# A two-layer encoder: the first layer's operands from a feature-major copy of x, first loads on two queues, first products k-tile by k-tile

## The chip, the core and the metric

The kernel runs on one core of a Trainium2 chip. The core's engines each take their own instruction stream in order and wait for one another through semaphores: PE (TensorE, the matrix engine, with PEld for its weight loads), DVE (VectorE), ACT (ScalarE), POOL (GpSimd) and SP (SyncE, which here only issues DMAs; ACT issues a few as well). The metric is the device time of one execution in microseconds. Before the change it is 609.68 us, the median of three runs (608.34 to 611.04).

## What is computed

The reference is two layers on 256 tokens of 1024 features, all float32. Layer 0 mixes tokens by differential attention, layer 1 by a sparse attention with an indexer; each is followed by a squared-ReLU MLP of width 4096. Only the start of layer 0 matters here:

```
for i in range(DEPTH):
    h = rms_norm(x, norm_mix[i])
    ...
        mix = diff_attention(h, diff_w_in[j], ...)   # q, k, v = split(h @ w_in); rms_norm and rotary on q, k
    x = x + mix
    x = x + sq_relu_mlp(rms_norm(x, norm_mlp[i]), mlp_w1[i], mlp_w2[i])
```

The kernel applies the row scale of rms_norm after the product with the weights, so the product itself needs only x times the gain of each feature, with features on partitions.

## The kernel before

**Split products.** Every float32 operand is split into a high part `hi` (a copy in the matrix engine's reduced format, on ACT, L146 for weights) and a remainder `lo` (on DVE, L147). `mm3` (L150 to L156) multiplies `hi*hi`, `hi*lo` and `lo*hi` into one accumulator, so each 128 x 128 piece of activations against 512 weight columns costs three matmuls (L151, L153, L155). They are called main matmuls below.

**Weights** come in units of 128 x 2048 numbers (1 MB): `unit` issues the DMA on SP and splits the unit in pieces. Three raw buffers and four split buffers rotate, so a DMA waits until DVE has split the unit that is three ahead. The units are called u0, u1, ... in the order of use.

**The start.** `make_h` transposes x, 128 x 128 at a time, on PE (L228, 16 of them), and ACT (L232) and DVE (L234) write the two halves of h from PSUM, times the feature gain. x arrives in four DMAs between the pieces of u0. Warm-up matmuls on zeros (`warm`, L91) run before and between. ACT's queue carries `pack` (gains, identity matrix, constants) and the positions `posi`.

**The first attention layer.** Four groups a0 to a3 of heads; each is one block of 48 main matmuls on two units (`project`: four k-tiles for the first 128 tokens, the same four for the others, then the second unit), followed by two blocks for v. The work on a group's result (`qk_post` and `diff_probs`) runs as a side job: sums of squares (ACT L366, DVE L367), rsqrt (L173 to L179), rotary (L352 to L355), transposes to qkT (PE L384), scores (PE L400, DVE L411), exponentials (ACT L422), difference of the two softmaxes (DVE L594), transposes to keys (PE L429), products with v (PE L436 to L438) and transposes to the next operand (PE L623, from `on`, ACT L618). The output projection begins with main matmul 289.

**Rotary angles** are a chain of some 40 tiny operations on POOL (`rope_angles`, L263 to L316). `rope_sines` takes their sines on ACT (L326 to L328), loads the table for the exponentials (L330) and so stands before every rsqrt of the layer.

**Row scale.** `row_scale` squares x on ACT (L200) and finishes on DVE.

**Order.** A scheduler sets the order of each engine's stream when the program is built; on the chip every engine takes its stream in order. So a change in the first block also shifts where later transposes stand among the main matmuls.

Of the kernel before, what the change touches and what calls it, by code (L numbers as in the profile page):

```python
# [9 lines left out]
F32 = mybir.dt.float32  # L10
F32R = mybir.dt.float32r
I32 = mybir.dt.int32
AF = mybir.ActivationFunctionType
OP = mybir.AluOpType
AX = mybir.AxisListType

D = 1024
# [8 lines left out]
C_NORM = 0  # L26
# [2 lines left out]
C_CQ = 37  # L29
C_ROPE = 40  # L30
C_INV = 120
C_ID = 128
C_LAM = 256
C_END = 512

INV_FREQ = [1.0, 0.1939227432012558, 0.03760603070259094, 0.007292664609849453,
            0.0014142135623842478, 0.00027424818836152554, 5.3182957344688475e-05, 1.0313385246263351e-05]
# [5 lines left out]


@with_exitstack
def trunk(ctx: ExitStack, tc: tile.TileContext, x_in, pos_in, pack_in, wf, out):
    nc = tc.nc
    E = ctx.enter_context
    const = E(tc.tile_pool(name="const", bufs=1))
# [8 lines left out]
    mm = nc.tensor.matmul  # L58
# [4 lines left out]
    def wk():  # L63
        return psum.tile([128, 512], F32, name="wk", bufs=4)


    x = [const.tile([128, D], F32, name=f"x{t}") for t in range(2)]
    pack = const.tile([128, C_END], F32, name="pack")
    posi = const.tile([128, 2], I32, name="posi")

    def load_x(t, n):
        nc.sync.dma_start(x[t][:, n * 512:(n + 1) * 512], x_in[t * 128:(t + 1) * 128, n * 512:(n + 1) * 512])

    nc.scalar.preload_act_table_set("trig_and_small")
    load_x(0, 0)
    nc.scalar.dma_start(pack[:, :C_LAM], pack_in[:, :C_LAM])
    nc.scalar.dma_start(posi, pos_in)

    ident = pack[:, C_ID:C_ID + 128]
    cmask = const.tile([128, 384], F32, name="cmask")  # L80
    vt = const.tile([128, 2, D], F32, name="vt")
    nc.vector.memset(vt[:, 0, :128], 0.0)
    nc.gpsimd.memset(cmask, 0.0)
    nc.gpsimd.memset(cmask[0:64, 64:128], BIG)
    nc.gpsimd.memset(cmask[0:64, 320:384], BIG)


    def warm(n):
        ps = wk()
        for _ in range(n):  # L90
            mm(ps[:, :128], vt[:, 0, :128], vt[:, 0, :128], start=True, stop=True)  # L91

    warm(7)


    def pause(stage):
# [31 lines left out]
    off = [0]  # L128
    split = []

    def unit(cols=2048, dmas=1, pieces=1, between=None):
        raw = wraw.tile([128, 2048], F32, name="raw")
        hi = wsp.tile([128, 2048], F32R, name="whi")
        lo = wsp.tile([128, 2048], F32R, name="wlo")
        src = bass.AP(tensor=wf.tensor, offset=wf.offset + off[0], ap=[[cols, 128], [1, cols]])
        off[0] += 128 * cols
        step = cols // dmas
        for i in range(dmas):
            c = slice(i * step, (i + 1) * step)
            nc.sync.dma_start(raw[:, c], src[:, c])  # L140
            if between is not None and i == 0:
                between()
        step = cols // pieces
        for i in range(pieces):
            c = slice(i * step, (i + 1) * step)
            split[:] = [nc.scalar.activation(hi[:, c], raw[:, c], AF.Copy).ins]  # L146
            nc.vector.tensor_tensor(lo[:, c], raw[:, c], hi[:, c].bitcast(F32), op=OP.subtract)  # L147
        return hi[:, :cols], lo[:, :cols]

    def mm3(ps, ah, al, wh, wl, first, last):  # L150
        mm(ps, ah, wh, start=first, stop=False)  # L151
        tick()
        mm(ps, ah, wl, start=False, stop=False)  # L153
        tick()
        mm(ps, al, wh, start=False, stop=last)  # L155
        tick()  # L156
# [62 lines left out]
    behind = []  # L219
# [16 lines left out]
    def lhs(h, kt, t):  # L236
        hi, lo = h[kt // 4][:2]
        c = slice(t * 128, t * 128 + 128)
        return hi[:, kt % 4, c], lo[:, kt % 4, c]

    def project(ps, h, parts, n):

        nk = sum(p[2] for p in parts)
        k0 = 0
        for wh, wl, cnt in parts:
            wh = wh.rearrange("p (k n) -> p k n", n=n)
            wl = wl.rearrange("p (k n) -> p k n", n=n)
            for t in range(2):
                for i in range(cnt):
                    k = k0 + i  # L250
                    ah, al = lhs(h, k, t)
                    mm3(ps[t], ah, al, wh[:, i], wl[:, i], k == 0, k == nk - 1)
            k0 += cnt

    def quad(us):
        return [(wh, wl, 4) for wh, wl in us]
# [5 lines left out]
    def rope_angles():  # L262
        ve = nc.gpsimd  # L263
        posf = const.tile([128, 2], F32, name="posf")
        ve.tensor_copy(posf, posi)
        shp = [128, 2, 8]
        ang = const.tile(shp, F32, name="ang")
        for t in range(2):
            ve.tensor_scalar(ang[:, t], pack[:, C_INV:C_INV + 8], posf[:, t:t + 1], None, op0=OP.mult)
        tp = const.tile(shp, F32, name="tp")  # L270
        n = const.tile(shp, F32, name="rn")
        nh = const.tile(shp, F32, name="rnh")

        def take(v, m, c):
            ve.tensor_scalar(tp, m, c, None, op0=OP.mult)  # L275
            ve.tensor_tensor(v, v, tp, op=OP.subtract)  # L276

        def whole(o, v, c):
            ve.tensor_scalar(o, v, c, RND, op0=OP.mult, op1=OP.add)
            ve.tensor_scalar(o, o, RND, None, op0=OP.subtract)  # L280

        two_pi = 2.0 * math.pi

        a2 = const.tile(shp, F32, name="a2")
        whole(a2, ang, 2.0 ** -24)
        take(ang, a2, 2.0 ** 24)

        c1 = math.floor(two_pi * 2 ** 9) / 2 ** 9
        c2 = math.floor((two_pi - c1) * 2 ** 21) / 2 ** 21
        whole(n, ang, 1.0 / two_pi)  # L290
        ve.tensor_scalar(nh, n, 1.0 / 2048, RND, op0=OP.mult, op1=OP.add)
        ve.tensor_scalar(nh, nh, RND, 2048.0, op0=OP.subtract, op1=OP.mult)
        nl = const.tile(shp, F32, name="rnl")
        ve.tensor_tensor(nl, n, nh, op=OP.subtract)
        for c in (c1, c2):
            take(ang, nh, c)
            take(ang, nl, c)
        take(ang, n, two_pi - c1 - c2)

        b1 = math.floor(two_pi * 2 ** 14) / 2 ** 14  # L300

        def wrap(v):
            whole(n, v, 1.0 / two_pi)
            take(v, n, b1)
            take(v, n, two_pi - b1)

        k24 = -0.8939688666801969
        kh = math.floor(k24 * 2 ** 12) / 2 ** 12
        b = const.tile(shp, F32, name="rb")
        ve.tensor_scalar(b, a2, kh, None, op0=OP.mult)  # L310
        wrap(b)
        ve.tensor_tensor(ang, ang, b, op=OP.add)
        take(ang, a2, kh - k24)
        wrap(ang)
        lim = 3.1415925
        ve.tensor_scalar(ang, ang, lim, -lim, op0=OP.min, op1=OP.max)  # L316
        return ang, b
# [212 lines left out]


    h = new_h()
    make_h(h, C_NORM, 0, 0)
    warm(4)
    ua = [unit(dmas=4, pieces=4, between=lambda: load_x(0, 1))]
    make_h(h, C_NORM, 0, 1)
    for n in range(2):
        load_x(1, n)
        make_h(h, C_NORM, 1, n)
    ua.append(unit(dmas=2, pieces=4))  # L540
    nc.sync.dma_start(pack[:, C_LAM:], pack_in[:, C_LAM:])
    srow, s2 = row_scale(1)
    angles = rope_angles()
    s2c = const.tile([128, 2], F32, name="s2c0")
# [85 lines left out]
    ready = []  # L630

    def pair():
        return [unit(pieces=2) for _ in range(2)]

    def take():
        return ready.pop(0) if ready else pair()
# [2 lines left out]
    probs, outs = [], []  # L639
    for j in range(4):  # L640
        ps = [acc() for _ in range(2)]
        project(ps, h, quad(take() if j else ua), 512)
        if j == 0:
            ready.append(pair())
            rope_sines(*angles)
            lam()
        probs.append(spawn(diff_probs(ps, pr[j], f"a{j}")))
# [5 lines left out]
    h = new_h()  # L653
# [3 lines left out]
    h = h1  # L657
# [184 lines left out]
def _tiles(w):  # L842

    k, n = w.shape[0] // 128, w.shape[1]
    return w.reshape(k, 128, n).transpose(1, 0, 2).reshape(-1)
# [48 lines left out]
def _pack(i):  # L894

    p = np.zeros((128, C_END), np.float32)
    for n, name in ((0, "norm_mix"), (1, "norm_mlp")):
        for layer in range(2):
            c = C_NORM + 16 * layer + 8 * n
            p[:, c:c + 8] = i[name][layer].reshape(8, 128).T  # L900
    heads = [i[n][0] for n in ("diff_q_norm", "diff_k_norm", "dsa_q_norm", "dsa_k_norm")]
    for c, g in enumerate(heads):
        for r in (0, 64):
            p[r:r + 16, C_GT + c] = 1.0
            p[r + 16:r + 64, C_GT + c] = g[16:]
        p[:, C_ROPE + 16 * c:C_ROPE + 16 * c + 16] = g[:16]
    p[:, C_ROPE + 64:C_ROPE + 80] = 1.0
    p[:, C_SUB] = i["diff_subln"][0]
    p[:, C_CQ:C_CQ + 2] = i["dsa_cq_norm"][0].reshape(2, 128).T
    p[:, C_INV:C_INV + 8] = np.array(INV_FREQ, np.float32)  # L910
    p[:, C_ID:C_ID + 128] = np.eye(128, dtype=np.float32)
    for n, name in enumerate(("q1", "k1", "q2", "k2")):
        p[:, C_LAM + 64 * n:C_LAM + 64 * n + 64] = i["diff_lam_" + name][0]
    return p
# [21 lines left out]
```

## Time and profile before

| what | value |
|---|---|
| median of three runs | 609.68 us (608.34 to 611.04) |
| the profiled execution | 610.02 us |
| its span, first to last instruction | 607.4 us |
| PE busy | 593.5 us |
| DVE, ACT, POOL busy | 428.1, 368.9, 19.1 us |

2.6 us of the profiled execution lie outside its span. Matmuls are pipelined, so a busy PE may still be slowed by what it waits for between two of them: the starts of successive matmuls tell more than the busy time. In the steady state main matmuls start 0.23 us apart. The chain that ended last follows the work back from the last instruction, at each step to what released it.

### The profile page before, as it was taken

To read this page: it belongs to the slowest core of one execution; us is meant where nothing else is said; L and a number is where in the kernel's file an instruction comes from. 1 tells how busy PE (TensorE), PEld (TensorE's weight loads), DVE (VectorE), ACT (ScalarE), POOL (GpSimd) and SP (SyncE) were. 2 spreads that over 40 slices of the span, in tenths; PEclk is the share of its full clock that TensorE was granted. 3 is DMA by queue.
4 is the path that set the end of the run, shared out by engine and by line. 5 is a ranking of instruction groups with operands and counts; after the bars stand their busy time and mean duration, and the time that the engine had idled before them with its cause. 6 is when DMAs were issued, how large, how long until landed. Compare 5 with 4: busy or idle time off the path is not lost.

```text
span 607.4 us, 8479 instructions
## 1 busy us (share of the span) xinstructions
PE 593.5 (98%) x3072; PEld 488.2 (80%) x3072; DVE 428.1 (70%) x1067; ACT 368.9 (61%) x720; POOL 19.1 (3%) x53
## 2 busy tenths in 40 slices
PE   8989999999999999999999899999999999999997
PEld 6767678888888888888787686778888888888886
DVE  5799986579557557656598999766786565666552
ACT  6789987576445444445397589784854454455430
POOL 5600000000000000000000000000000000000000
PEclk9999999999999999999999899999999999999999
DMA  8753453335645564555453226424465555555301
GB/s 311 261 207 145 143 199 132 146 139 209 208 169 183 203 201 161 193 208 169 162 208 140 71 69 209 139 69 140 139 240 185 199 208 177 179 199 206 141 1 70
DMA packets 16025, 102.29 MB, mean 168 GB/s; under 512 B 1904, under 2 KB 2416, under 8 KB 4336
## 3 DMA queue, kind: packets, MB, share of 16 engines
q1 hardware_dynamic: 15696, 101.62, 47.4%
q8 instruction: 24, 0.39, 0.3%
q10 hardware_dynamic: 288, 0.13, 0.1%
q14 instruction: 17, 0.14, 0.1%
HBM read 100.70 MB, written 1.05 MB: 168 GB/s over the span
## 4 chain that ended last, share of the span: by engine, by line
PE 81%; DVE 10%; ACT 3%; POOL 3%; issue 3%; DVEq 0%; POOLq 0%; ACTq 0%
PE wk L479 18%; PE acc L153 15%; PE acc L155 15%; PE acc L151 15%; PE wk L480 9%; DVE wlo L147 4%; DVE s L411 2%; PE wk L429 2%; PE acc L479 1%; PE wk L400 1%; PE wk L228 1%; POOL ang L276 1%; PE wk L384 1%; POOL tp L275 1%; ACT whi L146 1%
## 5 line engine op out<-in xcount | busy, mean ns | idle before, releaser
L147 DVE TENSOR_TENSOR wlo<-raw,whi 128x1024 fp32r<-128x1024 f32 (+2 forms) x210 | 230.0, 1116 | 115.7 <-ACT whi L146 115.5
L146 ACT ACTIVATE whi<-raw 128x1024 fp32r<-128x1024 f32 (+2 forms) x210 | 197.9, 975 | 96.2 <-issue 46.1
L153 PE MATMUL acc<-wlo,act 128*128 128x512 f32 (+1 forms) x504 | 198.8, 394 | 0.6 <-DVE wlo L147 0.6
L151 PE MATMUL acc<-whi,act 128*128 128x512 f32 (+1 forms) x504 | 199.1, 395 | 0.1
L155 PE MATMUL acc<-whi,act 128*128 128x512 f32 (+1 forms) x504 | 198.5, 394 | 0.0
L479 PE MATMUL wk<-act,whi 128*128 128x512 f32 x480 | 169.8, 398 | 0.0
L480 PE MATMUL wk<-act,wlo 128*128 128x256 f32 x480 | 134.7, 281 | 0.0
L155 PEld LDWEIGHTS acc<-whi,act 128*128 128x128 f32 x504 | 95.3, 189 | 19.9 <-issue 1.7
L153 PEld LDWEIGHTS acc<-wlo,act 128*128 128x128 f32 x504 | 95.4, 189 | 19.7 <-DVE wlo L147 1.3
L151 PEld LDWEIGHTS acc<-whi,act 128*128 128x128 f32 x504 | 95.2, 189 | 19.5 <-issue 1.0
L479 PEld LDWEIGHTS wk<-act,whi 128*128 128x128 f32 x480 | 90.1, 188 | 22.0
L480 PEld LDWEIGHTS wk<-act,wlo 128*128 128x128 f32 x480 | 90.7, 189 | 0.5
L488 ACT ACTIVATE act<-on 128x256 fp32r<-128x256 f32 x64 | 26.3, 417 | 57.5 <-DVE on L487 57.5
L422 ACT ACTIVATE s<-s,nb,rs_r 128x128 f32<-128x128 f32 x64 | 34.2, 537 | 6.0 <-DVE nb L420 5.9
L489 DVE TENSOR_TENSOR act<-on,act 128x256 fp32r<-128x256 f32 x64 | 26.8, 424 | 14.5 <-ACT act L488 12.7
L485 ACT ACTIVATE sq<-wk 128x256 f32<-128x256 f32 x60 | 22.4, 375 | 17.6 <-PE wk L480 17.6
L487 DVE SCALAR_TENSOR_TENSOR on<-sq 128x256 f32<-128x256 f32 x64 | 26.6, 421 | 0.9
L486 DVE TENSOR_TENSOR sq<-wk,sq 128x256 f32<-128x256 f32 x60 | 24.9, 418 | 0.0
L232 ACT ACTIVATE act<-wk,pack 128x128 fp32r<-128x128 f32 x64 | 18.5, 377 | 8.1 <-PE wk L228 8.0
L234 DVE SCALAR_TENSOR_TENSOR act<-wk,pack,act 128x128 fp32r<-128x128 f32 x64 | 17.7, 344 | 3.6 <-ACT act L232 3.6
L429 PE MATMUL wk<-pack,s 128*128 128x128 f32 x72 | 15.7, 290 | 2.5 <-DVE s L594 1.7
L527 DVE SCALAR_TENSOR_TENSOR x<-acc,rows,x 128x256 f32<-128x256 f32 x16 | 7.0, 479 | 15.0 <-PE acc L155 15.0
(176 smaller groups left out, 435.6 us busy)
## 6 DMA issues: line engine op xcount, KB each, us to landing
raw<-in_w SPq DMA_DIRECT2D x91, 1024.0 KB, 4.8
x<-in_x SPq DMA_DIRECT2D x4, 256.0 KB, 4.5
raw<-in_w SPq DMA_DIRECT2D x4, 256.0 KB, 5.2
raw<-in_w SPq DMA_DIRECT2D x2, 512.0 KB, 5.8
raw<-in_w SPq DMA_DIRECT2D x1, 984.0 KB, 4.6
raw<-in_w SPq DMA_DIRECT2D x1, 840.0 KB, 4.8
out_dram<-x SPq DMA_DIRECT2D x3, 256.0 KB, 2.0
out_dram<-x SPq DMA_DIRECT2D x2, 128.0 KB, 1.7
```

The lines of the kernel that those rows point to most:

```text
L146: split[:] = [nc.scalar.activation(hi[:, c], raw[:, c], AF.Copy).ins]
L147: nc.vector.tensor_tensor(lo[:, c], raw[:, c], hi[:, c].bitcast(F32), op=OP.subtract)
L151: mm(ps, ah, wh, start=first, stop=False)
L153: mm(ps, ah, wl, start=False, stop=False)
L155: mm(ps, al, wh, start=False, stop=last)
L422: nc.scalar.activation(p[:, TS[t]], s[:, TS[t]], AF.Exp, bias=nb[:, t:t + 1], scale=nsc[:, t:t + 1], accum_out=z[t])
L429: nc.tensor.transpose(pt[:, i * 128:(i + 1) * 128], p[:, i * 128:(i + 1) * 128], ident)
L479: mm(ps.rearrange("p (a b) -> p a b", b=256), wh[:, k, c], both[:, :, k % 4], start=k == 0, stop=False)
L480: mm(ps[:, 256:], wl[:, k, c], hi[:, k % 4], start=False, stop=k == 7)
L487: nc.vector.scalar_tensor_tensor(q, r, 0.0, r, op0=OP.max, op1=OP.mult)
L488: nc.scalar.activation(uh[:, m], q, AF.Copy)
L489: nc.vector.tensor_tensor(ul[:, m], q, uh[:, m].bitcast(F32), op=OP.subtract)
```

## The change

The host lays out a second copy of x by features (`in_xt`, k-tile after k-tile, 256 tokens each) and puts the positions into `pack`, whose part that is needed first shrinks to 130 columns (the identity follows later). `first_h` makes both halves of a k-tile of h straight from that copy in SBUF, one ACT and one DVE instruction for all 256 tokens (128 x 256), with no transposes; the copy lies in the buffer of `vt`, which is free until the v blocks. A quarter of u0 is loaded on ACT's queue, and the rest of u0, u1 and the copy alternate on SP's. The ACT split of each weight quarter is tied behind the activation of the same k-tile (`each`). `project` takes the first block k-tile by k-tile, both token halves of each. u2 (`ahead`) is requested before x itself, which now comes in two loads of 512 KB and is needed for its squares and for the residual only; then follow the rest of `pack` and u3.

```diff
-    nc.scalar.dma_start(pack[:, :C_LAM], pack_in[:, :C_LAM])
-    nc.scalar.dma_start(posi, pos_in)
+    xt = vt.rearrange("p a b -> p (a b)")
+    def load_xt(k0, k1):
+        nc.sync.dma_start(xt[:, k0 * 256:k1 * 256], xt_in[:, k0 * 256:k1 * 256])
+    load_xt(0, 2)
+    nc.scalar.dma_start(pack[:, :C_ID], pack_in[:, :C_ID])
...
-    warm(7)
+    for _ in range(8):
+        mm(ps[:, :128], zero, zero, start=True, stop=True)
...
+            with tc.issue_after(each(i)) if each is not None else ExitStack():
+                split[:] = [nc.scalar.activation(hi[:, c], raw[:, c], AF.Copy).ins]
...
+            for t, i in ([(t, i) for i in range(cnt) for t in range(2)] if by_k else
+                         [(t, i) for t in range(2) for i in range(cnt)]):
...
-    make_h(h, C_NORM, 0, 0)
-    warm(4)
-    ua = [unit(dmas=4, pieces=4, between=lambda: load_x(0, 1))]
-    make_h(h, C_NORM, 0, 1)
-    for n in range(2):
-        load_x(1, n)
-        make_h(h, C_NORM, 1, n)
-    ua.append(unit(dmas=2, pieces=4))
-    nc.sync.dma_start(pack[:, C_LAM:], pack_in[:, C_LAM:])
+    def first_h(k):
+        hi, lo, _ = h[k // 4]
+        v, g = xt[:, k * 256:(k + 1) * 256], pack[:, C_NORM + k:C_NORM + k + 1]
+        with tc.issue_after(split[0]) if split else ExitStack():
+            behind[:] = [nc.scalar.activation(hi[:, k % 4], v, AF.Copy, scale=g).ins]
+        nc.vector.scalar_tensor_tensor(lo[:, k % 4], v, g, hi[:, k % 4].bitcast(F32), op0=OP.mult, op1=OP.subtract)
+        return behind[0]
+    ua = [unit(dmas=((nc.scalar, 0, 1, None), (nc.sync, 1, 2, lambda: load_xt(2, 4)),
+                     (nc.sync, 2, 4, lambda: load_xt(4, 8))), pieces=4, each=first_h)]
+    ua.append(unit(dmas=((nc.sync, 0, 1, None), (nc.sync, 1, 2, None)), pieces=4, each=lambda i: first_h(4 + i)))
+    ahead = unit(pieces=2)
+    for t in range(2):
+        nc.sync.dma_start(x[t], x_in[t * 128:(t + 1) * 128, :])
+    nc.sync.dma_start(pack[:, C_ID:], pack_in[:, C_ID:])
...
-        project(ps, h, quad(take() if j else ua), 512)
+        project(ps, h, quad(take() if j else ua), 512, by_k=j == 0)
         if j == 0:
-            ready.append(pair())
+            ready.append([ahead, unit(pieces=2)])
```

Three places show how the streams move; the rows name line, operation, result and inputs, and lines after the change are three or eleven higher. First PE, from the warm-up into the first block. Before:

```order
L91 MATMUL wk<-vt 128x128 x7
L228 MATMUL wk<-pack,x_79 128x128 x4
L91 MATMUL wk<-vt 128x128 x4
L228 MATMUL wk<-pack,x_79 128x128 x4
L151 MATMUL acc<-whi,act 128x512
L153 MATMUL acc<-wlo,act 128x512
L155 MATMUL acc<-whi,act 128x512
```

PE at the same place, after:

```order
L93 MATMUL wk<-zero 128x128 x8
L154 MATMUL acc<-whi,act 128x512 x2
L156 MATMUL acc<-wlo,act 128x512
L158 MATMUL acc<-whi,act 128x512
```

The transposes are gone, here and between the next main matmuls, and the first two products serve both token halves from one weight piece.

Second ACT, from the end of x's squares (L200, after: L203) over the sines (L326, L329) to the first rsqrt of a0 (`rs_y`). Before:

```order
L200 ACTIVATE qn,rowss<-x_80 128x1024
L364 ACTIVATE qn<-acc 128x512
L146 ACTIVATE whi<-raw 128x1024 x2
L366 ACTIVATE sq<-qn 128x512
L364 ACTIVATE qn<-acc 128x512
L146 ACTIVATE whi<-raw 128x1024 x2
L326 ACTIVATE sn<-ang 128x2x8
L327 ACTIVATE rb<-ang 128x16
L366 ACTIVATE sq<-qn 128x512
L328 ACTIVATE cs<-rb,hp 128x2x8
L330 ACT_TABLE_LOAD
```

ACT at the same place, after:

```order
L149 ACTIVATE whi<-raw 128x1024 x2
L203 ACTIVATE qn,rowss<-x_79 128x1024
L203 ACTIVATE qn,rowss<-x_80 128x1024
L367 ACTIVATE qn<-acc 128x512 x2
L369 ACTIVATE sq<-qn 128x512 x2
L149 ACTIVATE whi<-raw 128x1024 x2
L329 ACTIVATE sn<-ang 128x2x8
L330 ACTIVATE rb<-ang 128x16
L331 ACTIVATE cs<-rb,hp 128x2x8
L333 ACT_TABLE_LOAD
```

Both token halves' copies and sums of squares now stand ahead of u3's split and of the sines; u2's split has moved ahead of x's squares.

Third PE at the end of the attention stage, around the transposes of `on` (L623, after: L634). Before:

```order
L623 MATMUL wk<-pack,on 128x128
L155 MATMUL acc<-whi,act 128x512
L623 MATMUL wk<-pack,on 128x128 x2
L151 MATMUL acc<-whi,act 128x512
L623 MATMUL wk<-pack,on 128x128 x2
L153 MATMUL acc<-wlo,act 128x512
L623 MATMUL wk<-pack,on 128x128
```

PE at the same place, after:

```order
L158 MATMUL acc<-whi,act 128x512
L634 MATMUL wk<-pack,on 128x128 x5
L439 MATMUL wk<-vt,aT 128x128
L634 MATMUL wk<-pack,on 128x128
L440 MATMUL wk<-vt,aT 128x128
L634 MATMUL wk<-pack,on 128x128 x2
```

They stood among the last eight main matmuls of the second v block, and stand behind all of them now. Main matmuls counted up to each helper: the first transposes of a0 move from 106 to 110, its scores from 117 to 122; scores and first keys of a3 from 243 and 262 to 254 and 268, its second keys from 265 to 276. Beyond the attention stage the streams are the same.

## Rows read from the trace of the kernel before

**Rows 1.** The page: the span, and the shares of the chain that ended last.

```profile
span 607.4 us, 8479 instructions
...
PE 81%; DVE 10%; ACT 3%; POOL 3%; issue 3%; DVEq 0%; POOLq 0%; ACTq 0%
```

**Rows 2.** Busy time by engine in stretches from the span's start (PE, PEld, DVE, ACT, POOL, with the number of instructions; then the granted clock, DMA share and GB/s).

```profile
30.00:50.00 20.00, 17.43 (x90) 13.43 (x90) 20.00 (x64) 17.83 (x37) 0.00 (x0) 1.00 0.60 220
...
130.00:140.00 10.00, 10.00 (x60) 8.81 (x60) 7.65 (x16) 7.79 (x16) 0.00 (x0) 1.00 0.60 210
```

**Rows 3.** What PE waited for between 7 and 100 us (us in total, times, longest).

```profile
PE wk L384 <- DVE qn L355: 2.2, 1, 2.2
PE wk L429 <- DVE s L594: 1.7, 4, 0.5
```

**Rows 4.** The timeline of PE (start, duration, instruction). Main matmuls 0, 14, 48, 49 and 105 by their place in the stream, then the first transposes of a0 and, behind main matmul 109, the next six.

```profile
7.10 0.48 PE L151 MATMUL acc<-whi,act 128*128 128x512 f32 x1
...
12.33 0.40 PE L155 MATMUL acc<-whi,act 128*128 128x512 f32 x1
...
20.15 0.39 PE L151 MATMUL acc<-whi,act 128*128 128x512 f32 x1
20.84 0.50 PE L153 MATMUL acc<-wlo,act 128*128 128x512 f32 x1 [0.30 <-DVE wlo L147]
...
33.68 0.39 PE L151 MATMUL acc<-whi,act 128*128 128x512 f32 x1
36.23 0.44 PE L384 MATMUL wk<-pack,qn 128*128 128x128 f32 x2 [2.16 <-DVE qn L355]
...
37.44 0.82 PE L384 MATMUL wk<-pack,qn 128*128 128x128 f32 x6
```

**Rows 5.** The chain that ended last, between 0 and 37 us (start, duration, what).

```profile
1.43 4.63 issue
...
10.79 0.22 POOL rnh L291
...
13.38 1.49 POOL ang L276
...
25.31 0.21 POOL ang L316
25.55 0.22 ACT sn L326
...
29.66 1.23 DVE wlo L147
```

**Rows 6.** The timeline of ACT: a square of x, the first half's sum of squares of a0, the split of u3, the sines.

```profile
13.63 1.07 ACT L200 ACTIVATE qn<-x 128x1024 f32<-128x1024 f32 x1
...
20.05 0.62 ACT L366 ACTIVATE sq<-qn 128x512 f32<-128x512 f32 x1
...
21.05 2.00 ACT L146 ACTIVATE whi<-raw 128x1024 fp32r<-128x1024 f32 x2
25.55 0.22 ACT L326 ACTIVATE sn<-ang 128x16 f32<-128x16 f32 x1 [2.50 <-POOL ang L316]
```

**Rows 7.** DMA issues (result, queue, number, KB each, us from issue to landing): the two on ACT's queue, issued at 0.75 and 1.18 us; the first quarter of u0, issued at 1.17 us; u2, issued at 7.66 us. Then what moved from 4 to 4.5 us and from 7 to 8 us.

```profile
pack<-in_pack ACTq DMA_DIRECT2D x1, 128.0 KB, 3.2
posi<-in_pos ACTq DMA_DIRECT2D x1, 1.0 KB, 4.9
...
raw<-in_w SPq DMA_DIRECT2D x1, 256.0 KB, 4.7
...
raw<-in_w SPq DMA_DIRECT2D x1, 1024.0 KB, 8.1
...
DMA packets 57, 0.06 MB, mean 123 GB/s; under 512 B 27, under 2 KB 27, under 8 KB 57
...
DMA packets 225, 0.40 MB, mean 404 GB/s; under 512 B 28, under 2 KB 28, under 8 KB 225
```

**Rows 8.** Groups of instructions in the first 20 us, shapes kept apart (number, then busy us and mean ns of one), with the 1024-column split from 7 to 35 us.

```profile
L146 ACT ACTIVATE whi<-raw 128x512 fp32r<-128x512 f32 x8 | 4.9, 641 | 3.9 <-DMA raw<-in_w 3.9
L147 DVE TENSOR_TENSOR wlo<-raw,whi 128x512 fp32r<-128x512 f32 x8 | 5.4, 692 | 3.1 <-ACT whi L146 3.0
L232 ACT ACTIVATE act<-wk,pack 128x128 fp32r<-128x128 f32 x16 | 5.0, 372 | 0.2
...
L147 DVE TENSOR_TENSOR wlo<-raw,whi 128x1024 fp32r<-128x1024 f32 x8 | 9.6, 1220 | 1.2 <-ACT whi L146 1.2
```

**Rows 9.** The timeline of PE at the end of the attention stage: scores of a3, its last key transposes, the first transposes of `on`, the last product with v.

```profile
80.77 1.58 PE L400 MATMUL wk<-qkT 64*128 64x128 f32 x16
...
88.89 0.44 PE L429 MATMUL wk<-pack,s 128*128 128x128 f32 x2
...
95.50 0.33 PE L623 MATMUL wk<-pack,on 128*128 128x128 f32 x1
...
100.81 0.39 PE L438 MATMUL wk<-vt,aT 128*128 128x128 f32 x2
```

**Rows 10.** The timeline of ACT there: the eight scalings that make `on`.

```profile
95.08 2.18 ACT L618 ACTIVATE on<-wk,rs_r 128x128 f32<-128x128 f32 x8
```

**Rows 11.** Busy time and granted clock (third number from the end) around the idle stretch of PE in the second layer, columns as in rows 2.

```profile
343.30:345.20 1.90, 0.00 (x0) 0.01 (x1) 1.90 (x11) 0.00 (x0) 0.00 (x0) 1.00 0.18 73
345.20:348.70 3.50, 3.47 (x10) 2.82 (x11) 3.50 (x14) 1.96 (x4) 0.00 (x0) 0.51 0.02 5
```

More of the change, by code (lines that the diff above doesn't have):

```diff
@@ L31 @@
 C_INV = 120
-C_ID = 128
-C_LAM = 256
-C_END = 512
+C_POS = 128
+C_ID = 130
+C_LAM = 258
+C_END = 514
 INV_FREQ = [1.0, 0.1939227432012558, 0.03760603070259094, 0.007292664609849453,
@@ L45, in trunk @@
 @with_exitstack
-def trunk(ctx: ExitStack, tc: tile.TileContext, x_in, pos_in, pack_in, wf, out):
+def trunk(ctx: ExitStack, tc: tile.TileContext, x_in, xt_in, pack_in, wf, out):
     nc = tc.nc
@@ L68, in trunk @@
     pack = const.tile([128, C_END], F32, name="pack")
-    posi = const.tile([128, 2], I32, name="posi")
-    def load_x(t, n):
-        nc.sync.dma_start(x[t][:, n * 512:(n + 1) * 512], x_in[t * 128:(t + 1) * 128, n * 512:(n + 1) * 512])
+    vt = const.tile([128, 2, D], F32, name="vt")
+    xt = vt.rearrange("p a b -> p (a b)")
+    def load_xt(k0, k1):
+        nc.sync.dma_start(xt[:, k0 * 256:k1 * 256], xt_in[:, k0 * 256:k1 * 256])
     nc.scalar.preload_act_table_set("trig_and_small")
-    load_x(0, 0)
-    nc.scalar.dma_start(pack[:, :C_LAM], pack_in[:, :C_LAM])
-    nc.scalar.dma_start(posi, pos_in)
+    load_xt(0, 2)
+    nc.scalar.dma_start(pack[:, :C_ID], pack_in[:, :C_ID])
     ident = pack[:, C_ID:C_ID + 128]
     cmask = const.tile([128, 384], F32, name="cmask")
-    vt = const.tile([128, 2, D], F32, name="vt")
-    nc.vector.memset(vt[:, 0, :128], 0.0)
+    zero = const.tile([128, 128], F32, name="zero")
+    nc.vector.memset(zero, 0.0)
     nc.gpsimd.memset(cmask, 0.0)
@@ L85, in trunk @@
     nc.gpsimd.memset(cmask[0:64, 320:384], BIG)
[L88 to L91, printed above, removed]
-    warm(7)
+    ps = wk()
+    for _ in range(8):
+        mm(ps[:, :128], zero, zero, start=True, stop=True)
     def pause(stage):
@@ L129, in trunk, with unit @@
     split = []
-    def unit(cols=2048, dmas=1, pieces=1, between=None):
+    def unit(cols=2048, dmas=((nc.sync, 0, 1, None),), pieces=1, each=None):
         raw = wraw.tile([128, 2048], F32, name="raw")
@@ L136, in unit @@
         off[0] += 128 * cols
[L137 to L142, printed above, removed]
+        step = cols // dmas[-1][2]
+        for queue, a, b, then in dmas:
+            c = slice(a * step, b * step)
+            queue.dma_start(raw[:, c], src[:, c])
+            if then is not None:
+                then()
         step = cols // pieces
@@ L145, in unit @@
             c = slice(i * step, (i + 1) * step)
-            split[:] = [nc.scalar.activation(hi[:, c], raw[:, c], AF.Copy).ins]
+            with tc.issue_after(each(i)) if each is not None else ExitStack():
+                split[:] = [nc.scalar.activation(hi[:, c], raw[:, c], AF.Copy).ins]
             nc.vector.tensor_tensor(lo[:, c], raw[:, c], hi[:, c].bitcast(F32), op=OP.subtract)
@@ L239, in lhs, with project @@
         return hi[:, kt % 4, c], lo[:, kt % 4, c]
-    def project(ps, h, parts, n):
+    def project(ps, h, parts, n, by_k=False):
         nk = sum(p[2] for p in parts)
@@ L247, in project @@
             wl = wl.rearrange("p (k n) -> p k n", n=n)
[L248 to L252, printed above, removed]
+            for t, i in ([(t, i) for i in range(cnt) for t in range(2)] if by_k else
+                         [(t, i) for t in range(2) for i in range(cnt)]):
+                k = k0 + i
+                ah, al = lhs(h, k, t)
+                mm3(ps[t], ah, al, wh[:, i], wl[:, i], k == 0, k == nk - 1)
             k0 += cnt
@@ L264, in rope_angles @@
         posf = const.tile([128, 2], F32, name="posf")
-        ve.tensor_copy(posf, posi)
+        ve.tensor_copy(posf, pack[:, C_POS:C_POS + 2].bitcast(I32))
         shp = [128, 2, 8]
@@ L909, in _pack @@
     p[:, C_CQ:C_CQ + 2] = i["dsa_cq_norm"][0].reshape(2, 128).T
+    p[:, C_POS:C_POS + 2] = np.ascontiguousarray(i["positions"][0].reshape(2, 128).T).view(np.float32)
     p[:, C_INV:C_INV + 8] = np.array(INV_FREQ, np.float32)
@@ L923 @@
         "in_x": np.ascontiguousarray(i["x"][0]),
-        "in_pos": np.ascontiguousarray(i["positions"][0].reshape(2, 128).T),
+        "in_xt": _tiles(i["x"][0].T).reshape(128, -1),
         "in_pack": _pack(i),
```

## The prediction

> **What bounds the kernel now.** I read the chain that ended last first: 81% of it is PE [rows 1], and from 100 us on PE has no gaps ([rows 2] shows 130 to 140 us). Beyond the attention stage the change moves nothing, so what it gains or loses must be there when main matmul 289 (output projection) starts, at about 101.1 us, just behind the last product with v [rows 9]. Before that point PE is not alone. The chain begins with 4.6 us in which POOL waits for the positions, goes through POOL's angle chain to 25.5 us, then through ACT's sines and the table load to a DVE split at 29.66 us [rows 5]. The sines kept ACT idle for 2.5 us [rows 6]. From 30 to 50 us DVE is busy all the time [rows 2], and PE waits for its results: 2.2 us at the first transposes of a0, 1.7 us in four key transposes [rows 3].
>
> **Where PE stands before.** Main matmul 14 starts at 12.33 us and 48 at 20.15 us [rows 4]: 7.82 us for 34, or 0.23 each. Counted back, the first block runs as if it had started without gaps at 12.33 - 14 x 0.23 = 9.1 us; the first really starts at 7.1 us and is held up by loads, splits and transposes. Main matmul 49 comes 0.69 us behind 48, so 0.46 us are lost there. Behind 105 (33.68 us) the transposes come at 36.23 us, 2.3 us later than a pace of 0.23 allows [rows 4].
>
> **Term 1, the first block: -3.1 us (-2.5 to -4.0).** The first product needs the first quarter of u0 and ACT's split of it (0.64 us [rows 8]). The quarter landed at 1.17 + 4.7 = 5.87 us [rows 7]. It is now issued at about 1.18 us, in the place of the positions, on a queue with only half of the former first load of `pack` ahead of it. Bounds: as late as before (first product at 5.87 + 0.64 + 0.1 = 6.6 us), or with the shortest latency in the trace, 3.2 us (5.1 us). Between them stands the rate: from 4 to 4.5 us only 123 GB/s move, with packets under 512 B, those of the positions, among them; later 404 [rows 7]. They are gone, so I take a landing at 5.3 and a start at 6.0 us: 9.1 - 6.0. From there a k-tile keeps PE busy for 6 x 0.23 = 1.4 us. ACT needs 0.64 plus about 0.45 (between the 128-column 0.37 and the 512-column 0.64), DVE 0.69 plus about 0.45 [rows 8], the DMAs 0.39 MB at 0.40 MB/us, about 1.0. All three fit beside PE, so 16 transposes and their 32 PSUM reads cost nothing any more.
> On the second queue the Trainium skill ("DMA: Bandwidth & Descriptors", Issuing engines are not separate DMA queues) says that DMAs from several engines share the same DMA engines and only issue time is saved. By that the term would be its lower bound, -2.5; no row here shows two queues with large loads.
>
> **Term 2, u3 behind x: +0.3 us (-0.5 to +1.3).** The copy and x together are 1 MB more in front of u3. u2 landed at 7.66 + 8.1 = 15.8 us before [rows 7]; I take 15.0 now. Then ACT splits it (2.0), squares x (2 x 1.05), copies and squares a0 (about 2.1) and reaches u3 at 21.2 us [rows 6]; u3 itself, 2.3 MB behind u2, should land at 20 to 21. The first `lo` is ready at 21.2 + 1.0 + 1.2 [rows 6, 8] = 23.4 us. PE asks for it behind main matmul 72, at 6.0 + 72 x 0.23 = 22.6 us. It loses 0.8 where it lost 0.46.
>
> **Term 3, the transposes of a0: -2.2 us (0 to -2.3).** POOL starts with `pack`, at 0.75 + 3.2 = 3.95 instead of 6.1 us [rows 5, 7], and ends by about 21.5 us: some 36 operations at 0.32 us, longer beside DVE splits. ACT reaches the sines only behind u3's split, at 23.2 us, against 25.55 [rows 6]. From there to the transposes it took 10.7 us. One sum of squares (0.5) stands ahead of the sines now and one pair of DVE splits (2 x 1.22 [rows 8]) behind a0's rotary; a sum over squares (0.6) and small waits come in. So some 8.8 us, to 32.0. PE arrives at 6.0 + 0.8 + 110 x 0.23 = 32.1 us. The wait is gone; next late are the keys.
>
> After these three PE is 3.1 - 0.3 + 2.2 = 5.0 us ahead.
>
> **Term 4, groups a0 to a2: +1.2 us (0 to +2.6).** DVE was saturated [rows 2], ACT nearly, and both have the same work with only 2.4 us of head start. I followed the new order with the old durations. PE waits before its key transposes 0.9, 0.3, 0.7 and 0.7 us, and some 0.5 us for ACT's copies of qkT; before, 1.25 us in the first three groups, 0.5 in the fourth [rows 3]. The helpers stand 4 to 15 main matmuls later, which absorbs the rest. The upper bound leaves PE only the sines' 2.4 us.
>
> **Term 5, the last group: +0.5 us (0 to +2.0).** From a3's scores to its last keys 8.1 us pass [rows 9], with 22 main matmuls before and after; two DVE splits no longer stand in between, and I take 7.3. From there to 101.1 us it takes 12.2 us with 23 main matmuls; now there are 12, which is 2.5 us less. But the transposes of `on` can begin only behind the whole second v block, the copy of v (0.6) and the first scaling (0.4), and come at ACT's pace of 2.18 us for eight [rows 10] with little PE work between: 1.3 us more, 11.0 in all. PE counts 11 main matmuls more at a3's scores, so -0.8 + 1.3 = 0.5 us are lost.
>
> **Sum.** -3.1 + 0.3 - 2.2 + 1.2 + 0.5 = -3.3 us. The profiled execution took 610.02 us, which gives 606.7; the median of the runs is 0.34 lower, and from it the forecast is 606.4 us.
>
> **The rivals.**
> *The whole lead is kept.* If the later places of the helpers cover DVE and ACT, terms 4 and 5 vanish: -5.0, 604.7 us. For it: 4 to 15 main matmuls of 0.23 are 0.9 to 3.4 us of cover. Against it: DVE at 20.00 of 20 us [rows 2].
> *The stage swallows the lead.* If DVE and ACT carry no more than the sines' 2.4 us through the stage and the transposes of `on` take another 1, -1.4 remains: 608.3 us.
> *POOL is held off.* One angle operation took 1.49 us, and it spans two splits, others 0.22 [rows 5]; in the first block DVE reads PSUM in 16 of its 24 instructions before, and SBUF alone in all 16 after. If POOL gets nothing between them, it has some 14 operations done at 18.3 us and ends at 26.4. The sines come 3.3 us later than forecast and PE's lead falls to 1.6, with term 5 to 1.1: 608.6 us. The Trainium skill ("SBUF — State Buffer", Who interferes with whom) says so: a DVE instruction with two SBUF inputs shuts out a GpSimd operation that reads SBUF for its whole length, one with a single SBUF input does not. The trace agrees for the splits; no row shows it for the new form.
> *The clock falls.* PE idles from about 4.7 to 6.0 us. In the second layer PE was idle for 1.9 us, and then the granted clock was 0.51 (the lower level, 1.2 GHz) for 3.5 us [rows 11], 1.7 us lost. The gap is shorter here, but with a late quarter it is as long: 608.1 us.
> *Slower than before.* If every angle operation between 5.4 and 18.3 us takes the worst 1.49 us [rows 5], 8 are done there instead of 26; with u3's two splits in the way too, POOL ends at 29.1 us. The sines are 5.9 us later than forecast and the lead becomes -0.9, with term 5 -1.4: 611.1 us. It decides from sines later than about 27.7 us.
>
> **How the numbers follow.** A measurement of this kernel tells about 0.5%, 3.05 us, from no change; the line lies at 606.6 us, close to my forecast. The forecast (607.4 to 605.4) has 50%, of which 33 lie beyond the line; the whole lead 20%; the swallowed lead 15%; POOL held off 7%; the clock 4%; slower 4%, half of it over 612.7. Faster 0.33 + 0.20 = 0.53, same 0.17 + 0.15 + 0.07 + 0.04 + 0.02 = 0.45, slower 0.02. The range reaches from 603.9 (whole lead, with term 1 near its upper bound) to 608.9 (POOL held off) and leaves out some 2 in 10.
>
> **What would show it.** Term 1: the first main matmul at 5.1 to 6.6 us and 48 at 16.7 to 17.7. Term 2: a wait for `lo` of u3 of 0.3 to 1.7 us near 22.6. Term 3: POOL's last angle before 22.5, the sines near 23.2, a0's transposes near 32. Terms 4 and 5: a3's scores near 79.5, main matmul 289 near 97.8 us. Wrong would be: sines behind POOL again, a first quarter that lands after 6.5 us, u3 after 23 us, or a granted clock below 1.00 in the first 20 us.

## The result, and the profile after

The changed kernel took **606.46 us** (median of 7 runs, 605.77 to 607.49), the kernel before 609.78 us (7 runs, 608.34 to 611.29): a ratio of 0.9948, with a 95% interval from 0.9929 to 0.9968. The profiled execution after took 606.46 us with a span of 604.3 us, against 610.02 and 607.4 us before [rows 1]. The forecast was 606.4 us. The number is right; the way to it, as the traces show, was not.

Products are counted here from one: "the 49th" is the one that the prediction, and the expectation of the first run, call 48. The 289th is the first of the output projection, the 469th lies in the first MLP. The page after, its span and the shares of the chain that ended last:

```profile
span 604.3 us, 8415 instructions
...
PE 84%; DVE 12%; ACT 2%; DMA 1%; issue 1%; DVEq 0%; ACTq 0%
```

POOL has left the chain (it had 3% [rows 1]), and PE's share is larger. What PE waited for between 7 and 100 us:

```profile
PE acc L154 <- ACT whi L149: 2.0, 1, 2.0
PE wk L432 <- DVE s L605: 1.3, 3, 0.5
PE wk L634 <- ACT on L629: 1.0, 1, 1.0
```

The 2.2 us before a0's transposes [rows 3] are gone. The key transposes cost 1.3 instead of 1.7 us, and the transposes of `on` a new 1.0. The first line is the gap ahead of the first product. PE's timeline from there on:

```profile
6.60 0.73 PE L154 MATMUL acc<-whi,act 128*128 128x512 f32 x2 [1.99 <-ACT whi L149]
7.33 0.54 PE L156 MATMUL acc<-wlo,act 128*128 128x512 f32 x1
...
8.09 0.63 PE L156 MATMUL acc<-wlo,act 128*128 128x512 f32 x1
8.52 0.63 PE L158 MATMUL acc<-whi,act 128*128 128x512 f32 x1
8.95 0.63 PE L154 MATMUL acc<-whi,act 128*128 128x512 f32 x1
9.37 0.63 PE L156 MATMUL acc<-wlo,act 128*128 128x512 f32 x1
...
11.31 0.40 PE L154 MATMUL acc<-whi,act 128*128 128x512 f32 x1
11.55 0.39 PE L156 MATMUL acc<-wlo,act 128*128 128x512 f32 x1
```

The first product starts at 6.60 us, the upper bound of term 1. From about 7.7 to 11.1 us the products start 0.43 us apart instead of 0.23. The next rows say why: busy time of PE in stretches, then the granted clock, the DMAs' share and GB/s.

```profile
7.00:9.00 2.00, 2.00 (x7) 0.66 1.00 387
9.00:11.00 2.00, 2.00 (x6) 0.50 1.04 426
11.00:13.00 2.00, 2.00 (x10) 0.98 1.04 436
```

The granted clock was 0.50 (1.2 GHz): PE had run warm-up products until 4.61 us and then been idle for 1.99. The rival that the prediction gave 4% happened, and with it one of its own signs of being wrong (a granted clock below 1.00 in the first 20 us), within a total that came out as forecast. On ACT, what it waited for at the start, and the sines:

```profile
4.75 0.51 ACT L542 ACTIVATE act<-vt,pack 128x256 fp32r<-128x256 f32 x1 [2.74 <-DMA pack<-in_pack]
5.92 0.63 ACT L149 ACTIVATE whi<-raw 128x512 fp32r<-128x512 f32 x1 [0.66 <-DMA raw<-in_w]
...
9.18 0.63 ACT L149 ACTIVATE whi<-raw 128x512 fp32r<-128x512 f32 x1 [1.32 <-DMA raw<-in_w]
...
21.52 2.00 ACT L149 ACTIVATE whi<-raw 128x1024 fp32r<-128x1024 f32 x2
23.41 0.20 ACT L329 ACTIVATE sn<-ang 128x16 f32<-128x16 f32 x1
```

The first quarter of weights was there at 5.9 us, as before, and the third only at 9.18. The sines stand directly behind u3's split and wait for nothing; before they waited 2.5 us for POOL [rows 6].

**Where the time came from.** Starts of the same products in the two traces:

| product | before, us | after, us | lead, us |
|---|---|---|---|
| 1st | 7.10 | 6.60 | 0.50 |
| 49th | 20.15 | 19.48 | 0.67 |
| 289th, first of the output projection | 100.95 | 98.16 | 2.79 |
| 349th | 115.58 | 113.10 | 2.48 |
| 469th, first MLP | 178.40 | 176.28 | 2.12 |
| 889th, second layer | 337.91 | 335.80 | 2.11 |
| 949th | 356.40 | 352.76 | 3.64 |
| 1069th | 406.03 | 402.83 | 3.20 |

The first layer gives 2.1 us; another 1.1 come between the 889th and the 1069th product, where the change moves nothing. There PE waits for its first transposes of the keys, 2.17 us in both traces. Before, the clock fell to 0.51 behind that wait [rows 11]; in this execution it did not. PE's timeline before, then after:

```profile
345.23 0.62 PE L384 MATMUL wk<-pack,qn 128*128 128x128 f32 x2 [2.17 <-DVE qn L355]
```

```profile
343.12 0.41 PE L387 MATMUL wk<-pack,qn 128*128 128x128 f32 x2 [2.17 <-DVE qn L358]
```

```profile
342.00:344.00 2.00, 0.88 (x5) 1.00 0.00 0
344.00:346.00 2.00, 2.00 (x10) 1.00 0.00 0
346.00:348.00 2.00, 2.00 (x13) 1.00 0.03 8
```

The wait is the same, the clock behind it not. Runs of one program differ too: of 60 further runs of the kernel before, 42 had a mean granted clock under 0.999, with a median of 610.1 us, and 18 did not, with 608.4. (The mean does not say where a run lost its clock.) In the eight variants below with 12 or more warm-up products it was 35 of 64, but between 1 of 6 (e6) and 10 of 12 (e11): that the change makes such a fall rarer is not shown.

For the attention stage a ledger can be kept: the start of the 289th product is that of the first, plus PE's busy time, plus its idle time between. That sum holds by construction; what tells something is which of the three has moved (busy and idle of each trace from the stretch between the two products):

| kernel | first product | busy | idle | 289th |
|---|---|---|---|---|
| before | 7.10 | 89.22 | 4.63 | 100.95 |
| after | 6.60 | 89.12 | 2.44 | 98.16 |
| after, 16 warm-up products | 7.55 | 87.39 | 2.53 | 97.47 |
| before, positions in `pack` | 7.22 | 89.02 | 2.63 | 98.87 |
| after, positions late | 6.63 | 89.89 | 4.06 | 100.58 |

From before to after 2.19 of the 2.79 us are idle time and 0.50 the earlier first product; the busy time hardly moves. The transposes of x are no longer in the busy time (1.9 us), and nine products at the lower clock have taken their place (9 x 0.2 = 1.8 us). The last three lines are experiments.

### The profile page after: what moved, and what is told of

Same layout as the page of the kernel before. It is cut to its first block, busy times and chain, and to the rows that moved or that the text cites. A ratio compares the mean times of both kernels' runs of the same rounds, so it can differ in the third digit from the quotient of the medians.

```text
span 604.3 us, 8415 instructions
## 1 busy us (share of the span) xinstructions
PE 591.5 (98%) x3050; PEld 486.5 (81%) x3050; DVE 426.8 (71%) x1059; ACT 367.4 (61%) x712; POOL 18.9 (3%) x53
## 4 chain that ended last, share of the span: by engine, by line
PE 84%; DVE 12%; ACT 2%; DMA 1%; issue 1%; DVEq 0%; ACTq 0%
PE wk L482 19%; PE acc L156 16%; PE acc L154 16%; PE acc L158 16%; PE wk L483 9%; DVE wlo L150 4%; PE wk L432 2%; DVE s L414 2%; PE acc L482 1%; PE wk L403 1%; PE wk L231 1%; DVE score L769 1%; DVE qkss L370 1%; DMA raw<-in_w 1%; DVE m L768 1%; DVE qn L377 1%
## 5 line engine op out<-in xcount | busy, mean ns | idle before, releaser
L235 ACT ACTIVATE act<-wk,pack 128x128 fp32r<-128x128 f32 x48 | 13.5, 378 | 8.0 <-PE wk L231 8.0
L432 PEld LDWEIGHTS wk<-pack,s 128*128 128x128 f32 x72 | 8.8, 140 | 9.8 <-DVE s L605 3.6
```

Source lines behind the costliest of these rows:

```text
L432: nc.tensor.transpose(pt[:, i * 128:(i + 1) * 128], p[:, i * 128:(i + 1) * 128], ident)
```

## The experiments

Two theories were set against each other. *S*: the stage is paced by ACT's and DVE's chain from the sines, and what PE does ahead of it is slack. *P*, later called the ledger: what PE loses or gains before the output projection it keeps. Each kernel was timed beside the kernel before (609.5 to 609.8 us in these series).

| run | 1st | 13th | 49th | 289th | 469th | median, us | ratio (95%) |
|---|---|---|---|---|---|---|---|
| e1_warm16 | 7.55 | 10.37 | 18.56 | 97.47 | 175.62 | 605.39 | 0.9931 (0.9919 to 0.9943) |
| e2_warm12 | 6.97 | 10.12 | 18.94 | 97.83 | 175.98 | 605.72 | 0.9941 (0.9928 to 0.9954) |
| e3_pos_late | 6.63 | 11.11 | 19.27 | 100.58 | 178.31 | 609.05 | 0.9994 (0.9984 to 1.0004) |
| e4_before_pos | 7.22 | 12.40 | 20.72 | 98.87 | 176.29 | 606.25 | 0.9950 (0.9937 to 0.9963) |
| e5_w16_tmajor | 7.12 | 10.92 | 19.11 | 97.90 | 176.01 | 606.35 | 0.9954 (0.9938 to 0.9970) |
| e6_w16_one_queue | 6.37 | 10.04 | 18.84 | 97.82 | 175.94 | 606.21 | 0.9948 (0.9928 to 0.9969) |
| e7_w14_quarters | 6.91 | 10.05 | 19.37 | 98.54 | 176.65 | 607.49 | 0.9962 (0.9948 to 0.9977) |
| e8_w16_sines_early | 7.20 | 10.12 | 18.50 | | 175.13 | 605.80 | 0.9940 (0.9919 to 0.9961) |
| e9_w14_sines_early | 6.53 | 9.70 | 18.51 | | 175.05 | 604.98 | 0.9933 (0.9915 to 0.9951) |
| e10_again | 6.87 | 11.30 | 19.79 | 98.61 | 176.77 | 606.79 | 0.9960 (0.9943 to 0.9976) |
| e11_w16_pos_own | 8.71 | 11.85 | 20.01 | 98.73 | 176.83 | 607.35 | 0.9970 (0.9956 to 0.9983) |

(In e8 and e9 the 289th product stands elsewhere among the products with v.) The 469th tells the first layer apart without the later clock. The medians bear it out where runs of like clock are compared: among those with a mean granted clock of 0.999 and above the median is 608.4 us before, 606.2 in e4 and 605.4 in e1, 2.2 and 3.0 us less, and the 469th product comes 2.1 and 2.8 us earlier.

**The clock in the first block.**

```diff
-    for _ in range(8):
+    for _ in range(16):
```

> Sixteen warm-up products in place of eight, so that TensorE is busy from 1.04 us almost to its first product at 6.60. Both theories: the granted clock stays at 1.00 from 7 to 11 us (it was 0.66 and 0.50 in the two stretches after the change), products 2 to 10 start 0.23 us apart, TensorE then waits about 0.5 us for the third quarter of the first unit, and product 48 starts at about 18.0 instead of 19.48. Theory S (the attention stage is paced by ScalarE's and VectorE's chain from the sines, and the 1.5 us that TensorE lost at the low clock were slack): a0's first transposes stay at 33.5, time 606.2 (606.0 to 606.5). Theory P (what TensorE loses in the first block it keeps to the end of the stage): transposes at 32.0, time 605.0 (604.7 to 605.3).

> Twelve warm-up products in place of eight: TensorE is idle for about 1.1 us before its first product instead of 1.99 us (the kernel before had idle 1.14 us there and a clock of 1.00 after it). If an idle stretch of 1.1 us is short enough, the granted clock stays at 1.00 and all is as with sixteen (theory S 606.2, theory P 605.0); if not, the clock falls as with eight and the time is 606.5.

With 16 and with 12 the granted clock stays at 1.00 (PE idle 0 and 1.39 us ahead of the first product). The 469th product comes 0.66 and 0.30 us earlier than after the change, the time falls by about 1.1 and 0.7. Theory S falls for this stretch: a0's transposes moved from 33.54 to 32.68 us. P is right in kind but too large: 0.92 us at the 49th product became 0.66 at the 469th. The warm-up products now ended at 7.55 us, later than the first split.

**The positions alone, both ways.**

```diff
-    ve.tensor_copy(posf, pack[:, C_POS:C_POS + 2].bitcast(I32))
+    ve.tensor_copy(posf, posi.bitcast(I32))
...
-    (nc.scalar, 0, 1, None)
+    (nc.scalar, 0, 1, lambda: nc.scalar.dma_start(posi, pack_in[:, C_POS:C_POS + 2]))
```

> The changed kernel with the positions in a transfer of their own behind the first quarter of weights on ScalarE's queue, so that GpSimd starts its angles at about 6.1 instead of 4.72; all else as after the change. Sines at about 24.8 instead of 23.41. Theory S: the stage shifts by the same 1.3 us, time 607.6 (607.2 to 607.9). Theory P: ScalarE does other work first and TensorE does not wait longer, time 606.6 (606.4 to 606.8).

The second is the kernel before with this one edit (the positions as two columns of `pack`):

```diff
-    nc.scalar.dma_start(posi, pos_in)
...
-    ve.tensor_copy(posf, posi)
+    ve.tensor_copy(posf, pack[:, C_POS:C_POS + 2].bitcast(I32))
```

> The kernel before with one edit: the positions travel in the first load of constants, as in the changed kernel, so that GpSimd starts its angles at about 4.0 instead of 6.06 and the sines run at about 23.5 instead of 25.55. Its start, its transposes of x and its order of loads are those of before. Theory S: most of the change's gain comes by this alone, time 607.7 (607.2 to 608.2). Theory P: the wait before a0's transposes shrinks by what the sines gain, but the first block is as late as before, time 609.0 (608.5 to 609.6).

These two settle where the gain comes from. The kernel before with the positions moved has nearly the whole gain: 469th product at 176.29 us against 176.28 after the full change, 606.25 us. The change without the early positions has none of it that can be told from noise: 609.05 us. That the positions alone carry most of it is what S said of e4. Both theories had the sizes wrong, in e3 because the 1 KB transfer took 5.8 us to land and not about 4.9: POOL started at 7.50 us, and ACT waited again. On ACT's and PE's timelines of e3:

```profile
26.62 0.22 ACT L330 ACTIVATE sn<-ang 128x16 f32<-128x16 f32 x1 [3.10 <-POOL ang L320]
```

```profile
31.63 0.50 PE L157 MATMUL acc<-wlo,act 128*128 128x512 f32 x1 [0.76 <-DVE wlo L151]
...
35.39 0.44 PE L388 MATMUL wk<-pack,qn 128*128 128x128 f32 x2 [0.35 <-DVE qn L359]
```

Sines 3.2 us later than after the change cost 2.0 us at the 469th product; sines 2.0 us earlier than before (23.53 us in e4) gave 2.1. In e4 PE's idle time falls by 2.0 us, and that is nearly all:

```profile
PE wk L428 <- DVE s L593: 1.3, 3, 0.5
PE acc L152 <- DVE wlo L146: 0.6, 2, 0.4
PE acc L150 <- ACT whi L145: 0.6, 1, 0.6
```

The transposes of x and the loads of x and of weights are still those of before.

**The parts of the new first block, with the clock kept.** Order of the products:

```diff
-    project(ps, h, quad(take() if j else ua), 512, by_k=j == 0)
+    project(ps, h, quad(take() if j else ua), 512, by_k=False)
```

> The kernel with sixteen warm-up products (605.39 us), and block 0's products again one token tile after the other (all four k of the first tile, then of the second) instead of k by k. Ledger theory (start of product 289 = start of product 1, plus TensorE's busy time, plus its idle time before it; busy time is the same in every kernel at the full clock): products 7 and 10 now wait for the third and fourth quarter of the first unit, of which the second low part was written at about 11.3, so about 1.2 us of idle time is added in the first block and none is saved later: product 289 at 98.7 instead of 97.47, time 606.6 (606.2 to 606.9). Theory S (ScalarE's and VectorE's chain from the sines has slack ahead of it): a0's transposes wait for that chain anyway, time 605.6 (605.3 to 605.9).

The 289th product is 0.43 us later than in e1 (the ledger said 1.2), the 469th 0.39; the median is 1.0 us higher, 0.7 among runs with a mean granted clock of 0.999 and above. That is the ledger's direction, at about a third of its size. From 9 to 11 us PE is busy for 1.68 us, with a wait for a split, where it was busy for 2.00 us in e1; the scheduler put some products of the second tile ahead of the late quarters by itself. The queue of the first quarter:

```diff
-    dmas=((nc.scalar, 0, 1, None),
+    dmas=((nc.sync, 0, 1, None),
```

> The kernel with sixteen warm-up products, and the first quarter of the weights issued from SyncE behind the first part of x by features instead of from ScalarE: one queue instead of two. If the two queues bring the first quarter earlier: it lands 0.3 to 0.7 us later than 5.9, and with TensorE busy with warm-up products until 7.55 that is hidden: 605.4 (605.2 to 605.7). If the queue of issue makes no difference: it lands within 0.2 us of where it was, 605.4 too; the landing of the first quarter and ScalarE's first split tell the two apart, not the time.

Neither expectation: on SyncE's queue alone the quarter came earlier. ACT's timeline:

```profile
4.53 0.51 ACT L542 ACTIVATE act<-vt,pack 128x256 fp32r<-128x256 f32 x1 [2.53 <-DMA pack<-in_pack]
5.01 0.63 ACT L149 ACTIVATE whi<-raw 128x512 fp32r<-128x512 f32 x1
...
9.36 0.63 ACT L149 ACTIVATE whi<-raw 128x512 fp32r<-128x512 f32 x1 [1.46 <-DMA raw<-in_w]
```

The split starts at 5.01 us without a wait; with two queues it waited until 6.01 (e1). The third quarter, which PE needs from its 13th product on, came 0.38 us later instead (8.98 in e1); the 15th product starts at 11.10 us (10.83 in e1), and 0.3 us are lost at the 469th. The Trainium skill ("DMA: Bandwidth & Descriptors", Issuing engines are not separate DMA queues) says that transfers from several engines share the same DMA engines and save only time of issue. The trace agrees: the second queue exchanged one landing for another.

```diff
-    (nc.sync, 2, 4, lambda: load_xt(4, 8))
+    (nc.sync, 2, 3, None), (nc.sync, 3, 4, lambda: load_xt(4, 8))
```

> Fourteen warm-up products (so that they end at about 6.6 instead of 7.55 and the first product is not held up), and the second half of the first unit as two transfers of a quarter each, so that the third quarter lands at about 8.4 instead of 9.18. Ledger theory: first product at 6.7, at most 0.3 us of idle time at product 13, all else as with sixteen; product 289 at 96.9, time 604.8 (604.5 to 605.2). Theory S: no gain, 605.4.

A miss: the third quarter landed at 9.37 us, not 8.4, although less was ahead of it, and what came behind was later too. On ACT's timeline of e7 the first split of the next unit (11.53 us in e1):

```profile
12.61 0.63 ACT L149 ACTIVATE whi<-raw 128x512 fp32r<-128x512 f32 x1 [0.77 <-DMA raw<-in_w]
```

The 469th product is 1.0 us later than in e1. Between 6 and 10 us 302 GB/s moved against 375 in e1. Why two transfers of 256 KB moved less than one of 512 KB is open.

**Earlier sines still, and the best version.**

```diff
-    ready.append([ahead, unit(pieces=2)])
-    rope_sines(*angles)
+    ready.append([ahead, unit(pieces=2, each=sines_between)])
```

(`sines_between` issues the sines and the table load ahead of the second piece.)

> The kernel with sixteen warm-up products, and the sines with their table load ahead of the second half of u3's split instead of behind it: sines at about 22.5 instead of 23.19, u3's second high part at 24.4 instead of 22.25. Ledger theory: a0's transposes did not wait with the sines at 23.19, so earlier sines bring nothing there, and TensorE now waits about 0.9 us for u3's second half: 606.2 (605.6 to 606.5). Theory S: the stage runs 0.7 us earlier, 604.7.

> Fourteen warm-up products, the first unit's loads as in the changed kernel (no further quarters), and the sines ahead of u3's second half. Ledger theory: product 13 is bound by the third quarter (landing at 9.0, split by 9.65) and starts at 10.05 as it did with the one queue; product 469 at 175.2 (it was 176.28 after the change, 175.62 with sixteen warm-up products, 175.36 with the early sines), time 605.2 (604.8 to 605.6).

PE did not wait for u3 in either, so the ledger's 0.9 us was wrong. On ACT's timelines the sines of e1, then of e8:

```profile
23.19 0.21 ACT L329 ACTIVATE sn<-ang 128x16 f32<-128x16 f32 x1
```

```profile
22.71 0.22 ACT L329 ACTIVATE sn<-ang 128x16 f32<-128x16 f32 x1 [0.34 <-POOL ang L319]
```

They run 0.48 us earlier, and the 469th product comes 0.49 us earlier than in e1, in e9 0.57: S's direction, nearly us for us. But the wait for `on` is gone there and the key transposes wait 2.2 to 2.3 us, with another order of the products with v, so that the sines alone did it is not shown. e9 is the fastest that was run, 604.98 us; its 13th product starts at 9.70, still bound by the third quarter.

**The change once more, and an own transfer for the positions.**

> The changed kernel once more, unedited, for a second trace of it beside these. Whether products 2 to 10 run at the lower clock again, in the granted clock or without it; product 469 near 176.3 if they do, near 175.6 if they do not; time 606.4 (606.0 to 606.9).

PE was idle for 2.04 us, and the clock fell again (0.73 from 8 to 9 us, 0.50 from 9 to 11). The 469th product at 176.77 and 606.79 us are the change's result again.

```diff
     nc.scalar.dma_start(pack[:, :C_ID], pack_in[:, :C_ID])
+    nc.scalar.dma_start(posi, pack_in[:, C_POS:C_POS + 2])
```

> The kernel with sixteen warm-up products, and the positions in a transfer of their own between the constants and the first quarter of weights, as in the kernel before: the new start at the full clock without the early angles. GpSimd starts at about 6.1, the sines run at about 25.3 instead of 23.19. Ledger theory: a0's transposes come 2.1 us later than 32.68 and that is TensorE's idle time, little of it given back: product 469 at 177.6 (it is 178.40 before and 175.62 with the early angles), time 607.4 (606.9 to 608.0). If the new start alone carries the gain: product 469 at 175.7, time 605.5.

This did not test what it was made for: POOL started 0.8 us later than in e1, but the sines ran at 23.64 us, since they stand behind u3's split anyway. The small transfer held up the quarter behind it on ACT's queue instead:

```profile
8.02 0.63 ACT L151 ACTIVATE whi<-raw 128x512 fp32r<-128x512 f32 x1 [2.68 <-DMA raw<-in_w]
```

That is 2.0 us later than in e1, the 13th product 1.48, the 49th 1.45, the 469th 1.21: a delay of PE in the first block, of which more than four fifths are kept. Theory S has room for 0.45 us of it, by which the sines came later (23.19 in e1); the ledger has room for all of it.

So neither theory holds alone. What PE loses ahead of a0's transposes it mostly keeps (e1, e11), and late sines cost it as well (e3, against e4).

## Why the prediction was right, and where it was not

**What held.** PE is the bound, and POOL's angles behind the positions cost its 2.2 us of idle time. Term 3 (-2.2) is the gain: POOL ended at 22.58 us, the sines ran at 23.41 (forecast 23.2), the wait before a0's transposes is gone (they stood at 33.54 us and not near 32, since PE itself came later), and e4 has -2.11 at the 469th product from this edit alone.

**Term 1 (-3.1) failed.** By its own formula the 15th product, at 11.78 us, gives an effective start of 8.56 us instead of 6.0: -0.54. Three steps broke. The quarter did not land at 5.3 us but at 5.9, behind `pack` on ACT's queue; one queue had it by 5.0 (e6). The low rate that the prediction blamed was gone from 4 to 4.5 us, but from 3 to 3.5 us only 45 GB/s moved, where 375 did before. The two stretches after, in that order of time:

```profile
DMA packets 17, 0.02 MB, mean 45 GB/s; under 512 B 0, under 2 KB 8, under 8 KB 17
...
DMA packets 124, 0.21 MB, mean 416 GB/s; under 512 B 12, under 2 KB 26, under 8 KB 124
```

The quarter landed as before; what held it is open. Next, "From there a k-tile keeps PE busy" took the later loads to fit beside PE, but the third quarter came at about 9.0 us, and with the clock kept the 13th product starts at 9.7 to 10.4 us, though the first starts anywhere from 6.37 to 7.55 (e1, e6, e7, e9). And the clock fell. That rival had the mechanism, with 1.7 us; without the fall the kernel gains 0.66 us at the 469th product (e1), since loads would have held PE up in part of that time.

**Term 2 (+0.3)** measured -0.46: no wait for u3, also with PE 0.9 us earlier (e1). **Terms 4 and 5 (+1.7)**: after terms 1 to 3 as measured the lead is 0.54 + 0.46 + 2.2 = 3.2 us, at the 289th product 2.79, so they cost 0.4. PE had less lead to lose, and a3's scores stood at 79.29 us (forecast 79.5). Of the forecast for the 289th product, 97.8 us, 0.36 is missing.

**"Beyond the attention stage the change moves nothing"** failed twice. From the 289th to the 469th product 0.67 us are given back: 0.31 before the 349th, where the transposes of `on` take 1.5 instead of 1.2 us among the products, and 0.36 behind it, where pairs of the MLP's products take 0.353 instead of 0.347 us without a wait. That slower stretch is in the changed kernel and its variants except e3; its cause is open. And the second layer gave 1.1 us that no term has, by a clock that falls behind the same wait in some runs and not in others. So -2.1 and not -3.3 us is what the change does in the first layer.

**That the total met the forecast is luck.** Against the forecast, term 1 lost 2.6 us and 0.7 were given back; term 2 won 0.8, terms 4 and 5 won 1.3, and 1.1 came from a clock that fell in the one execution and not in the other. They cancel to 0.1.

**The POOL rival** had a true mechanism. Operations beside DVE's instructions with two SBUF inputs were stretched, free ones were not; two of POOL's timeline after, the first beside a split:

```profile
6.59 0.81 POOL L278 TENSOR_SCALAR tp<-a 128x16 f32<-128x16 f32 x1
...
19.78 0.25 POOL L278 TENSOR_SCALAR tp<-a 128x16 f32<-128x16 f32 x1
```

The angles took 17.9 us (4.72 to 22.58) against 16.0 in e4 (3.94 to 19.92), where the halves of h still come from PSUM. That agrees with the Trainium skill ("SBUF — State Buffer", Who interferes with whom). The price was too high; DVE itself was busy for only 2.24 of 4 us from 6 to 10 us, as it waited for loads and splits. It cost nothing, as u3's split ended later than the angles.

## What to carry to other kernels

Before a large rewrite of a start, move the one transfer that the chain begins with: here two columns in another load gave the whole first-layer gain. Keep a ledger of the bounding engine (first instruction, busy, idle), and do not take it for a forecast: removed work shows up as gain only if nothing, such as a lower clock or the next load, fills its place. A total that comes out as forecast proves nothing; compare the starts of the same instructions at several places, those behind the change too.

## What was not expected of the hardware

The granted clock of the page does not show every stretch at the lower rate. In e3 the first products started 0.43 us apart, as after the change, yet the clock reads 1.00 from 6 to 10 us:

```profile
6.63 1.22 PE L155 MATMUL acc<-whi,act 128*128 128x512 f32 x2 [1.81 <-ACT whi L150]
7.65 0.63 PE L157 MATMUL acc<-wlo,act 128*128 128x512 f32 x1
8.08 0.63 PE L159 MATMUL acc<-whi,act 128*128 128x512 f32 x1
8.51 0.63 PE L157 MATMUL acc<-wlo,act 128*128 128x512 f32 x1
```

```profile
6.00:10.00 4.00, 3.37 (x8) 1.00 0.98 371
```

The first record of the clock in that trace stands at 10.17 us, where the spacing goes back to 0.23; ahead of it the view prints 1.00 with nothing to go by. The mean clock of that execution reads 1.000 all the same, so such a mean can miss a fall at the start. Read the spacing of equal products as well. And a transfer of 1 KB can be dear: 5.8 us to land behind 256 KB (e3), and 2.0 us more for the quarter that stands behind it (e11).
